# A hybrid decoder trunk: set-up sums kept in PSUM, a second raw weight buffer, GLA's score products in one run, later turns

## The chip, the cores and the metric

The kernel runs on one core of a Trainium2 chip. The metric is the device time of one execution, in microseconds (us). Each execution ends with the same output; the median of three is given, and one further execution was recorded by the hardware profiler. Engines are named as in the profile: PE (TensorE matmul), PEld (its weight loads), DVE (VectorE), ACT (ScalarE), POOL (GpSimd), SP (SyncE, which here issues most DMAs).

## The reference

One layer of a decoder trunk over 1024 tokens of width 1024, with four token mixers side by side on one normalised input:

```python
cond = jax.nn.silu(c)
shift, scale, gate = jnp.split(cond @ ada_w[l] + ada_b[l], 3, axis=-1)
u = _rms_norm(x, norm_g[l]) * (1 + scale[:, None]) + shift[:, None]
p = u @ w_in[l]
...
y_a = _rwkv7(...)     # A: delta-rule state update
y_b = _gla(...)       # B: gated linear attention
y_c = _mlstm(...)     # C: matrix memory
y_d = _hgrn2(...)     # D: gated linear recurrence
ys = jnp.stack([y_a * jax.nn.silu(rw_z), y_b * jax.nn.silu(gz),
                y_c * jax.nn.silu(mz), y_d * jax.nn.silu(hz)], axis=2).astype(dt)
branch = jnp.einsum('bsmv,mvd->bsmd', ys, w_branch[l])
gates = jax.nn.sigmoid(merge_logits).reshape(merge_logits.shape[:-1] + (N_BRANCH, D_MODEL))
merged = jnp.einsum('bsmd,bsmd->bsd', gates.astype(dt), branch)
x = x + gate[:, None] * (merged @ w_out[l])
return _rms_norm(x, final_g)
```

B and D share a chunked recurrence: per step S_t = diag(exp(log_g_t)) S_{t-1} + k_t v_t^T and o_t = S_t^T q_t. B (GLA) has 4 heads with keys of 64 and values of 128.

## The kernel before

Products in fp32 precision are made from three single-pass products: a weight `raw` tile is loaded, split by ACT into a rounded part `whi` (L303) and by DVE into the rest `wlo` (L304), and `mm3` (L314 to L316) issues hi x hi, hi x lo and lo x hi with 512 columns each. `project` does one 128-wide strip of `w_in` this way: 8 slices of 128 rows, 3 products each, for both halves of the sequence, 48 products in all. The raw tile has one buffer (`wraw`, L293, filled by SP at L297); `whi` and `wlo` have two each.

The program has these stages. **Set-up** (`make_u`, L153): x is normalised and transposed; then, for each of 8 slices j, `gather` (L220) forms the conditioning sums for shift and scale on DVE, as 8 operations on 128x256 tiles (L227 and L229) over `adaw`, which SP loads (L178). The sums of even and odd k go to two SBUF accumulators, four one-column products (L244) add them over partitions, L247 and L248 finish the slice's factors `ada` and `sD`, ACT makes `u` and its rounded part (L251, L252), POOL the rest `ul` (L253), and `chunk` multiplies the first two weight strips by it. Small parameter rows (`prow`, L107) are loaded meanwhile from ACT's queue, five behind each slice, and turned on PE at the end (L118, in `consts2`).

**Part one** is RWKV-7 (A), about 72 to 650 us, where SP first has sixteen loads `xd` (L385) that wait for a tile that POOL fills. **Part two** runs the units d0, b0, d1, c0, d2, b1, d3, c1 (HGRN2, GLA, mLSTM), each in four quarters of 256 tokens, with the projections of the next unit and gate projections between them, 650 to about 1490 us. Then come the merge and the output.

A quarter of a D or B unit first turns its values (`turn`, L922: PE transposes L927 into PSUM, ACT copies L932), forms the decayed keys `kt` in `carried` (ACT exponent, DVE L846), and turns those as well into `kT`. Products of `kT` and the values (L988 in D, L1131 in B) give what the chunk adds to the state. Then there are seven levels s = 64, 32, 16, 8, 4, 2, 1: ACT and DVE make a factor `lx`, DVE multiplies it by q (L1142 in B) and by k (L1145). For each chunk of 128 tokens PE then forms seven score products (L1154 in B, L1000 in D) and one for the tokens' own terms (L1156), DVE merges them into `AT` (L1162), and PE forms the output from the state (L1167) and from `AT` (L1171).

Which instruction comes next on an engine is decided by the Tile scheduler when the program is built: it orders each engine's stream by data and buffers, in program order where nothing else decides. `together` (L1302) emits a list of products with high priority and ties the later ones to the first, so that they stand as one run on PE. RWKV's scores (L619, L632) and D's scores are issued so; GLA's are not.

Of the kernel before, what the change touches and what calls it, by code (L numbers as in the profile page):

```python
# [18 lines left out]
P = 128  # L19
# [16 lines left out]
class Hybrid:  # L36
# [44 lines left out]
    def consts(self, sp):  # L81
# [17 lines left out]
        for name, ap, n in rows:  # L99
            if name in ("c", "mu"):  # L100
                o0, pr = o, sp.tile([P, P], F32, name=f"prow{o}")
            self.prow[name] = o
            if name == "conv":
                src = ap[0].rearrange("k (n p) -> (k n) p", p=P)
            else:
                src = ap.rearrange("a (n p) -> (a n) p", p=P)
            load = lambda d=pr[o - o0 : o - o0 + n, :], src=src: nc.scalar.dma_start(d, src)  # L107
            load() if o0 == 0 else self.loads.append(load)
            o += n
            if name == "ada_b":  # L110
                self.pturn(pr, 0, o)
# [41 lines left out]
    def make_u(self, first):  # L153
# [15 lines left out]
        for j in range(KC):  # L169

            if j in (1, 2):
                raw = self.wp.tile([P, KC, P], F32, tag="wraw", bufs=1, name="wraw0") if j == 1 else sp.tile([P, KC, P], F32, name="wraw1")
# [68 lines left out]
        for j in range(KC):  # L241
            for s in range(2):
                for z in range(2):
                    nc.tensor.matmul(aps[:, 8 * s + j : 8 * s + j + 1], lhsT=acc[z][:, s, :], rhs=self.one[:], start=z == 0, stop=z == 1)  # L244
# [14 lines left out]
            for _ in range(5):  # L259
                if self.loads:  # L260
                    self.loads.pop(0)()
# [7 lines left out]
    def gate_col(self, j):  # L269

        nc = self.nc
        w = self.wp.tile([P, KC, P], F32, tag="wraw", bufs=1, name=self.nm("gw"))
# [247 lines left out]
    def a_front(self, p, q):  # L520

        nc = self.nc
        r, k, v = (self.ast[p][n, q // 2][:, self.qsl(q)] for n in "rkv")
# [98 lines left out]
        self.together([lambda j=j, h=h: score(j, h) for j in range(4) for h in range(2)])  # L622
# [13 lines left out]
        self.together([lambda i=i: early(i // 2 % 2, 1 - i // 4, i % 2) for i in range(8)])  # L636
# [200 lines left out]
    def carried(self, c128, k):  # L837
# [9 lines left out]
        return f, self.turn(kt, "kT")  # L847
# [74 lines left out]
    def turn(self, src, name, cols=P, dst=None):  # L922
# [3 lines left out]
        for t in range(2):  # L926
            nc.tensor.transpose(pv[:, t * P : (t + 1) * P], src[:, t * P : (t + 1) * P], self.ident[:])  # L927
# [39 lines left out]
    def d_quarter(self, hd, qi, q, k, lg, v, sz, S):  # L967
# [4 lines left out]
        f, kT = self.carried(c128, k)  # L972
# [5 lines left out]
        for s in self.LV:  # L978
            x = self.level_factor(s, cs, lg)
            sp = lambda t: t[:, :QT].rearrange("p (b z t) -> p b z t", z=2, t=s)  # L980
            nc.vector.tensor_tensor(sp(x)[:, :, 1, :], sp(x)[:, :, 1, :], sp(q)[:, :, 1, :], ALU.mult)
# [134 lines left out]
    def b_quarter(self, pr, qi, q, k, lg, v, sz):  # L1116
# [3 lines left out]
        f, kT = self.carried(c128, k)  # L1120
# [6 lines left out]
        ps_ = self.iv()  # L1127
        for c in range(2):
            for h in range(2):
                hr = slice(64 * h, 64 * h + 64)  # L1130
                nc.tensor.matmul(ps_[hr, c * P : (c + 1) * P], lhsT=kT[:, c * P + 64 * h : c * P + 64 * h + 64],  # L1131
                                 rhs=V[h][:, c * P : (c + 1) * P], start=True, stop=True)
        Z, R = [], []
        for s in self.LV:
# [5 lines left out]
            for h in range(2):  # L1140
                hr = slice(64 * h, 64 * h + 64)
                nc.vector.tensor_tensor(r[hr, :, h, :].rearrange("p c (b t) -> p c b t", t=s), s5(x)[hr, :, :, 1, :],  # L1142
                                        s5(q)[hr, :, :, 1, :], ALU.mult)
# [5 lines left out]
        for c in range(2):  # L1149
            cc = slice(c * P, (c + 1) * P)  # L1150
            sc = [self.sc() for _ in range(2)]
            for li, s in enumerate(self.LV):
                lhs = (k if s == 1 else Z[li])[:, cc]
                nc.tensor.matmul(sc[li // 4][:, P * (li % 4) : P * (li % 4) + P], lhsT=lhs,  # L1154
                                 rhs=R[li][:, c].rearrange("p h t -> p (h t)"), start=True, stop=True)
            nc.tensor.matmul(sc[1][:, 384:386], lhsT=dg[:, cc], rhs=self.bo2[:], start=True, stop=True)  # L1156
# [145 lines left out]
    def together(self, fs):  # L1302

        with self.tc.high_priority():
            first = fs[0]()
            with self.tc.issue_after(first.ins):
                for f in fs[1:]:
                    f()

# [124 lines left out]
    def bload(self, m, d):  # L1434
# [3 lines left out]
        raw = self.wp.tile([P, KC, P], F32, tag="wraw", bufs=1, name=self.nm("wraw"))  # L1438
# [145 lines left out]

YT = 11
# [42 lines left out]
```

## Time and profile before

| what | value |
| --- | --- |
| median of 3 executions | 1787.57 us (1785.57 to 1788.39) |
| the profiled execution | 1786.18 us |
| its span in the trace | 1784.4 us |
| PE busy | 1695.0 us, 95% of the span |
| DVE, ACT, POOL busy | 65%, 42%, 19% |
| mean granted TensorE clock | 0.981 |
| read and written in HBM | 111.88 and 33.56 MB |

The profiled execution took 1.39 us less than the median. Its span ends 1.8 us short of its own time; the difference lies around the span. Busy shares are means over stages: PE is busy nearly everywhere but in the first 110 us, so what an edit is worth is read from the gaps of PE in the stage where the edit lies. The granted clock is 1.00 at PE's full speed.

### The profile page before, as it was taken

To read this page: it belongs to the slowest core of one execution; us is meant where nothing else is said; L and a number is where in the kernel's file an instruction comes from. 1 tells how busy PE (TensorE), PEld (TensorE's weight loads), DVE (VectorE), ACT (ScalarE), POOL (GpSimd) and SP (SyncE) were. 2 spreads that over 40 slices of the span, in tenths; PEclk is the share of its full clock that TensorE was granted. 3 is DMA by queue.
4 is the path that set the end of the run, shared out by engine and by line. 5 is a ranking of instruction groups with operands and counts; after the bars stand their busy time and mean duration, and the time that the engine had idled before them with its cause. 6 is when DMAs were issued, how large, how long until landed. Compare 5 with 4: busy or idle time off the path is not lost.

```text
span 1784.4 us, 28695 instructions
## 1 busy us (share of the span) xinstructions
PE 1695.0 (95%) x10515; PEld 1356.6 (76%) x10515; DVE 1164.9 (65%) x3173; ACT 753.7 (42%) x1780; POOL 330.3 (19%) x555
## 2 busy tenths in 40 slices
PE   5989999999999999999899999999899999999998
PEld 4767677777777778787677877887678888778886
DVE  7756868667667744856878545666887654576532
ACT  5633343343344336546534453546543443222221
POOL 4621111111111121000110001000010020276500
PEclk7989999999999999999999999999999999999999
DMA  9222222222221221221221212111112225676322
GB/s 298 59 75 46 52 71 73 50 70 57 60 77 43 66 66 48 60 66 39 57 60 42 77 39 74 60 54 39 57 36 62 60 75 182 225 232 193 136 91 75
DMA packets 224278, 147.30 MB, mean 83 GB/s; under 512 B 60511, under 2 KB 203018, under 8 KB 224138
## 3 DMA queue, kind: packets, MB, share of 16 engines
q1 hardware_dynamic: 208800, 109.23, 22.5%
q10 hardware_dynamic: 15338, 36.24, 5.7%
q8 instruction: 83, 1.36, 0.3%
q14 instruction: 57, 0.47, 0.1%
HBM read 111.88 MB, written 33.56 MB: 82 GB/s over the span
## 4 chain that ended last, share of the span: by engine, by line
PE 70%; DVE 15%; ACT 6%; POOL 3%; DMA 3%; issue 3%; SPq 0%; POOLq 0%; ACTq 0%; DVEq 0%
PE pj L314 13%; PE pj L315 13%; PE pj L316 13%; PE yw L738 3%; PE sc L689 3%; DMA wraw<-in_w_in_dram 2%; DVE adacc L229 2%; PE sc L1000 1%; PE pj L1472 1%; PE pj L1470 1%; PE pj L1471 1%; PE iv L1471 1%; PE iv L1472 1%; PE iv L1470 1%; DVE tm L676 1%
## 5 line engine op out<-in xcount | busy, mean ns | idle before, releaser
L314 PE MATMUL pj<-uh,whi 128*128 128x512 f32 x1344 | 547.0, 407 | 3.9 <-DVE rn L534 3.8
L315 PE MATMUL pj<-ul,whi 128*128 128x512 f32 x1344 | 540.6, 402 | 0.0
L316 PE MATMUL pj<-uh,wlo 128*128 128x512 f32 x1344 | 540.6, 402 | 0.0
L314 PEld LDWEIGHTS pj<-uh,whi 128*128 128x128 f32 x1344 | 255.4, 190 | 51.2 <-issue 5.5
L316 PEld LDWEIGHTS pj<-uh,wlo 128*128 128x128 f32 x1344 | 255.0, 190 | 48.4 <-issue 2.0
L315 PEld LDWEIGHTS pj<-ul,whi 128*128 128x128 f32 x1344 | 255.5, 190 | 45.7 <-issue 1.2
L303 ACT CAST whi<-wraw 128x1024 fp32r<-128x1024 f32 x89 | 93.0, 1045 | 227.0 <-PE pj L315 177.4
L304 DVE TENSOR_TENSOR wlo<-wraw,whi 128x1024 fp32r<-128x1024 f32 (+1 forms) x88 | 106.9, 1215 | 45.9 <-ACT whi L303 41.6
L888 POOL TENSOR_SCALAR ss<-ss 128x2 f32<-128x2 f32 x48 | 13.3, 278 | 565.7 <-ACT on L887 564.1
L676 DVE TENSOR_TENSOR tm<-nb,xr 32x1 f32<-32x1 f32 (+14 forms) x240 | 71.7, 299 | 5.8
L897 DVE SCALAR_TENSOR_TENSOR y<-yw,DV,z 128x256 f32<-128x256 f32 x48 | 22.2, 480 | 63.3 <-PE yw L895 62.9
L1416 ACT ACTIVATE g<-pj 128x512 f32<-128x512 f32 x64 | 38.0, 594 | 54.2 <-PE pj L316 46.0
L678 DVE TENSOR_REDUCE xr<-tm 32x1 f32<-32x1 f32 (+14 forms) x240 | 54.0, 225 | 6.4
L1480 POOL TENSOR_TENSOR acc<-acc,g 128x512 f32<-128x512 f32 x32 | 50.5, 1589 | 24.3 <-DVE g L1478 21.1
L535 POOL TENSOR_TENSOR rn<-rn,nhalf 128x4 f32<-128x4 f32 x16 | 19.6, 1222 | 178.7 <-DVE rn L534 178.7
L751 DVE SCALAR_TENSOR_TENSOR Gbd<-Gbd,fa,yw 64x64 f32<-64x64 f32 x128 | 35.6, 278 | 25.7 <-PE yw L738 23.9
L1471 PE MATMUL iv<-yt,whi 128*128 128x512 f32 x128 | 50.4, 394 | 1.6 <-DVE yt L1430 1.6
L1470 PE MATMUL iv<-yt,whi 128*128 128x512 f32 x128 | 50.2, 392 | 1.5 <-DVE acc L1475 0.7
L1470 PE MATMUL pj<-yt,whi 128*128 128x512 f32 x128 | 50.4, 394 | 0.0
L1471 PE MATMUL pj<-yt,whi 128*128 128x512 f32 x128 | 50.3, 393 | 0.0
L1472 PE MATMUL pj<-yt,wlo 128*128 128x512 f32 x128 | 50.2, 393 | 0.0
L1472 PE MATMUL iv<-yt,wlo 128*128 128x512 f32 x128 | 50.1, 391 | 0.0
(483 smaller groups left out, 3399.9 us busy)
## 6 DMA issues: line engine op xcount, KB each, us to landing
wraw<-in_w_in_dram SPq DMA_DIRECT2D x89, 512.0 KB
gdram<-g ACTq DMA_DIRECT2D x64, 256.0 KB
th<-gdram ACTq DMA_DIRECT2D x32, 512.0 KB
adaw<-in_ada_w_dram SPq DMA_DIRECT2D x16, 512.0 KB
ydram<-y SPq DMA_DIRECT2D x64, 128.0 KB
wraw<-in_w_branch_dram SPq DMA_DIRECT2D x16, 512.0 KB
yr<-ydram SPq DMA_DIRECT2D x32, 256.0 KB
x<-in_x_dram SPq DMA_DIRECT2D x8, 512.0 KB
```

The lines of the kernel that those rows point to most:

```text
L303: nc.scalar.copy(hi[:, :nk, :width], raw[:, :nk, :width])
L304: eng.tensor_tensor(lo[:, :nk, :width], raw[:, :nk, :width], hi[:, :nk, :width].bitcast(F32), ALU.subtract)
L314: nc.tensor.matmul(ps[:width, :], lhsT=a, rhs=xh[:, k, :], start=k == 0, stop=False)
L315: nc.tensor.matmul(ps[:width, :], lhsT=a, rhs=xl[:, k, :], start=False, stop=False)
L316: nc.tensor.matmul(ps[:width, :], lhsT=b, rhs=xh[:, k, :], start=False, stop=k == nk - 1)
L676: nc.vector.tensor_tensor(t2, n2[:, 0:i, i].unsqueeze(1).broadcast_to([32, i, i]), x2[:, 0:i, 0:i].rearrange("p j l -> p l j"), ALU.mult)
L678: nc.vector.reduce_sum(x2[:, i, 0:i], t2, axis=AX.X)
L689: mm = lambda o, l, r: nc.tensor.matmul(o, lhsT=l, rhs=r, start=True, stop=True)
L738: mm = lambda o, l, r, **kw: nc.tensor.matmul(o, lhsT=l, rhs=r, skip_group_check=True, **kw)
L1470: nc.tensor.matmul(pb[:], lhsT=bh[:, k, :], rhs=t[:, 0, :], start=k == 0, stop=False)
L1471: nc.tensor.matmul(pb[:], lhsT=bh[:, k, :], rhs=t[:, 1, :], start=False, stop=False)
L1472: nc.tensor.matmul(pb[:], lhsT=bl[:, k, :], rhs=t[:, 0, :], start=False, stop=k == 3)
```

## The change

Six things are altered.

1. `gather` keeps one accumulator per slice, in a PSUM bank, through seven operations; the eighth writes the sum to SBUF. Each operation then reads what the one before it wrote. Two one-column products per slice are left of four.
2. Every `wraw` tile has two buffers, where before there was one. The scratch for dynamic DMAs is cut from 1024 to 256.
3. The 14 parameter rows after the first three are loaded from SP's queue, behind the last `adaw`.
4. In D and B, `carried` returns the keys unturned. They are turned when the product of the level s = 32 has been emitted, and `behind` orders the turn after that product (for the schedule alone: nothing waits in the program for it). In B the four state products move along.
5. GLA's seven score products of a chunk and the one for own terms go through `together`, in reversed order: s = 1 first, s = 64 last.
6. RWKV's first two fronts are no longer tied (`TIE`).

```diff
@@ consts
-            load = lambda d=pr[o - o0 : o - o0 + n, :], src=src: nc.scalar.dma_start(d, src)
-            load() if o0 == 0 else self.loads.append(load)
+            load = lambda q, d=pr[o - o0 : o - o0 + n, :], src=src: q.dma_start(d, src)
+            load(nc.scalar) if o0 == 0 else self.loads.append(load)
@@ make_u, behind the loads of adaw
+        for load in self.loads:
+            load(nc.sync)
@@ gather
-                self.acc = [sp.tile([P, 2, P], F32, tag=f"adacc{z}", bufs=2, name=f"adacc{z}{j}") for z in range(2)]
+                self.acc = self.iv()[:, 0 : 2 * P].rearrange("p (s c) -> p s c", s=2)
+            acc = self.acc
             for k in ks:
-                w, acc = aw[j][:, k], self.acc[k % 2]
-                if k < 2:
-                    nc.vector.tensor_scalar(acc[:], w, self.cond[:, k : k + 1], None, ALU.mult)
-                else:
-                    nc.vector.scalar_tensor_tensor(acc[:], w, self.cond[:, k : k + 1], acc[:], ALU.mult, ALU.add)
-            return self.acc
+                w = aw[j][:, k]
+                if k == 0:
+                    nc.vector.tensor_scalar(acc, w, self.cond[:, k : k + 1], None, ALU.mult)
+                    continue
+                o = acc
+                if k == KC - 1:
+                    o = sp.tile([P, 2, P], F32, tag="adacc", bufs=2, name=f"adacc{j}")
+                nc.vector.scalar_tensor_tensor(o if k < KC - 1 else o[:], w, self.cond[:, k : k + 1], acc, ALU.mult, ALU.add)
+            return o
@@ make_u, column products
-                for z in range(2):
-                    nc.tensor.matmul(aps[:, 8 * s + j : 8 * s + j + 1], lhsT=acc[z][:, s, :], rhs=self.one[:], start=z == 0, stop=z == 1)
+                nc.tensor.matmul(aps[:, 8 * s + j : 8 * s + j + 1], lhsT=acc[:, s, :], rhs=self.one[:], start=True, stop=True)
...
-            for _ in range(5):
-                if self.loads:
-                    self.loads.pop(0)()
@@ wraw (also gate_col, bload and make_u's first strip)
-        raw = self.wp.tile([P, KC, P], F32, tag="wraw", bufs=1, name=self.nm("wraw"))
+        raw = self.wp.tile([P, KC, P], F32, tag="wraw", bufs=2, name=self.nm("wraw"))
@@ a_front
+        tie = (p, q) >= TIE
-        self.together([lambda j=j, h=h: score(j, h) for j in range(4) for h in range(2)])
+        self.together([lambda j=j, h=h: score(j, h) for j in range(4) for h in range(2)], tie)
@@ carried
-        return f, self.turn(kt, "kT")
+        return f, kt
@@ turn
+            i = nc.tensor.transpose(pv[:, t * P : (t + 1) * P], src[:, t * P : (t + 1) * P], self.ident[:])
+            if after is not None:
+                self.behind(i, after)
@@ d_quarter and b_quarter, in the loop over levels
+            if s == 32:
+                kT = self.turn(kt, "kT", after=i)
@@ b_quarter: the four state products stand there too, and the scores
-            for li, s in enumerate(self.LV):
-                lhs = (k if s == 1 else Z[li])[:, cc]
-                nc.tensor.matmul(...)
-            nc.tensor.matmul(sc[1][:, 384:386], lhsT=dg[:, cc], rhs=self.bo2[:], start=True, stop=True)
+            self.together([lambda li=li, s=s: level(li, s) for li, s in reversed(list(enumerate(self.LV)))] + [own])
@@ together and behind
+    def together(self, fs, tie=True):
+        with self.tc.high_priority() if tie else ExitStack():
             first = fs[0]()
+            with self.tc.issue_after(first.ins) if tie else ExitStack():
                 for f in fs[1:]:
                     f()
+    def behind(self, ins, other):
+        self.tc.add_manual_dep(ins.ins, other.ins.name,
+                               mybir.DependencyInfo(mybir.DependencyClass.NoSync, mybir.DependencyReason.DATA), reason="behind")
@@ constants
+TIE = (0, 2)
-    nc = _bacc.Bacc("TRN2", target_bir_lowering=False, num_devices=1, dynamic_dma_scratch_size=1024)
+    nc = _bacc.Bacc("TRN2", target_bir_lowering=False, num_devices=1, dynamic_dma_scratch_size=256)
```

What the scheduler makes of it is shown at three places. A row is a line of the program, an operation, and its output and inputs by name with a serial number; lines are 1 to 27 higher in the changed program.

The first place is SP's queue behind the set-up, before. `wraw_783` and `wraw_848` are the strips of the first RWKV projections, the sixteen `xd` loads wait for POOL, and `wraw_1072` is the next strip:

```order
L297 DMA wraw_783<-in_w_in_dram 128x8x128
L297 DMA wraw_848<-in_w_in_dram 128x8x128
L1038 DMA mlb<-in_ml_i_b_dram 4x1
L396 DMA up_729<-in_rw_w_up_dram 64x512 x2
L396 DMA up_738<-in_rw_a_up_dram 64x512 x2
L385 DMA xd_700<-NT_690 128x128 x8
L385 DMA xd_701<-NT_690 128x128 x8
L297 DMA wraw_1072<-in_w_in_dram 128x8x128
```

After, where the rows ahead of these are the 14 `prow` loads:

```order
L299 DMA wraw_767<-in_w_in_dram 128x8x128
L299 DMA wraw_832<-in_w_in_dram 128x8x128
L299 DMA wraw_1056<-in_w_in_dram 128x8x128
L1045 DMA mlb<-in_ml_i_b_dram 4x1
L398 DMA up_713<-in_rw_w_up_dram 64x512 x2
L398 DMA up_722<-in_rw_a_up_dram 64x512 x2
L387 DMA xd_684<-NT_674 128x128 x8
L387 DMA xd_685<-NT_674 128x128 x8
L299 DMA wraw_1482<-in_w_in_dram 128x8x128
```

The third strip has moved ahead of the sixteen loads that wait for POOL; the fourth one, `wraw_1482`, now stands right behind them.

The second place is PE in the first quarter of a GLA unit (`pj` rows are projections of the next unit, `iv` takes transposes and state products, `sc` scores), before:

```order
L315 MATMUL pj_9039<-ul_75,whi_9036 128x512
L316 MATMUL pj_9039<-uh_73,wlo_9035 128x512
L927 MATMUL iv_8896<-ident,kt_8890 128x128 x2
L314 MATMUL pj_9039<-uh_73,whi_9036 128x512
L315 MATMUL pj_9039<-ul_75,whi_9036 128x512
L316 MATMUL pj_9039<-uh_73,wlo_9035 128x512
L1131 MATMUL iv_8910<-V_8883,kT_8899 64x128
L1131 MATMUL iv_8910<-V_8888,kT_8899 64x128
L1131 MATMUL iv_8910<-V_8883,kT_8899 64x128
L1131 MATMUL iv_8910<-V_8888,kT_8899 64x128
L314 MATMUL pj_9039<-uh_73,whi_9036 128x512
L1167 MATMUL yw_8984<-Sbd_8308,qe_8905 128x256
```

Further on, still before, the score products stand singly between projections:

```order
L1154 MATMUL sc_8965<-Zr_8291,lx_8938 128x128
L316 MATMUL pj_9081<-uh_74,wlo_9035 128x512
L314 MATMUL pj_9081<-uh_74,whi_9036 128x512
L1154 MATMUL sc_8966<-Zr_8292,lx_8945 128x128
L315 MATMUL pj_9081<-ul_76,whi_9036 128x512
L1154 MATMUL sc_8966<-Zr_8293,lx_8952 128x128
L316 MATMUL pj_9081<-uh_74,wlo_9035 128x512
L1154 MATMUL sc_8966<-Zr_8294,k_8185 128x128
L1156 MATMUL sc_8966<-bo_584,dg_8908 128x2
```

After, at the same quarter's scores:

```order
L316 MATMUL pj_9065<-uh_74,whi_9020 128x512
L1163 MATMUL sc_8950<-Zr_8278,k_8169 128x128
L1163 MATMUL sc_8950<-Zr_8277,lx_8936 128x128
L1163 MATMUL sc_8950<-Zr_8276,lx_8929 128x128
L1163 MATMUL sc_8949<-Zr_8275,lx_8922 128x128
L1163 MATMUL sc_8949<-Zr_8274,lx_8915 128x128
L1163 MATMUL sc_8949<-Zr_8273,lx_8896 128x128
L1163 MATMUL sc_8949<-Zr_8272,lx_8889 128x128
L1167 MATMUL sc_8950<-bo_568,dg_8887 128x2
L317 MATMUL pj_9065<-ul_76,whi_9020 128x512
```

The eight products of the chunk stand in one run that begins with s = 1. Counted from the transposes of the values, the keys' turn stands behind 22, 20, 32 and 19 products of 512 columns in the four quarters of b0 where it stood behind 12, 11, 20 and 13, and the own product behind 40, 39, 51 and 38 where it stood behind 33, 37, 40 and 34. On PE, about 2018 rows in a row, which hold all of RWKV, are in the same order as before.

The third place is ACT ahead of the first mLSTM quarter (`fa`, `fc` and `dk` belong to the projection of the D unit d2, and `g` is a gate), before:

```order
L945 ACTIVATE fa_11232<-fa_11232 128x512
L949 ACT_TABLE_LOAD
L949 ACTIVATE fa_11232<-fa_11232 128x512
L948 ACT_TABLE_LOAD
L948 ACTIVATE fc_11233<-fc_11233 128x512
L950 ACT_TABLE_LOAD
L950 ACTIVATE fc_11233<-fc_11233,lbt 128x512
L952 ACT_TABLE_LOAD
L952 ACTIVATE dk_11235<-dk_11235 128x512
L1416 ACTIVATE g_11279<-pj_11254 128x512
```

After:

```order
L950 ACTIVATE fa_11216<-fa_11216 128x512
L953 ACTIVATE fc_11217<-fc_11217 128x512
L954 ACT_TABLE_LOAD
L954 ACTIVATE fa_11216<-fa_11216 128x512
L955 ACTIVATE fc_11217<-fc_11217,lbt 128x512
L957 ACT_TABLE_LOAD
L957 ACTIVATE dk_11219<-dk_11219 128x512
L1435 ACTIVATE g_11263<-pj_11238 128x512
```

Two of four table loads are gone there. In the whole program ACT has 29 of them where before there were 35.

## Rows read from the trace of the kernel before

**Rows 1.** The page, busy time, share and instructions of each engine.

```profile
PE 1695.0 (95%) x10515; PEld 1356.6 (76%) x10515; DVE 1164.9 (65%) x3173; ACT 753.7 (42%) x1780; POOL 330.3 (19%) x555
```

**Rows 2.** Waits of PE: engine, line, releaser: us in total, times, longest us.

```profile
PE sc L244 <- DVE adacc L229: 14.3, 5, 5.5
PE iv L927 <- DVE kt L846: 9.1, 9, 1.7
PE iv L1131 <- ACT kT L932: 4.2, 2, 2.2
PE pj L314 <- DVE rn L534: 3.8, 1, 3.8
```

**Rows 3.** Waits of ACT.

```profile
ACT whi L303 <- PE pj L315: 177.4, 57, 5.1
```

**Rows 4.** Windows: stretch, its length, each engine's busy us and instructions, granted clock, DMA.

```profile
26.95:63.07 36.12, 27.29 (x118) 22.67 (x119) 35.85 (x69) 20.68 (x30) 20.53 (x14) 0.74 0.64 163
63.07:72.55 9.48, 9.48 (x37) 7.60 (x36) 3.32 (x17) 3.75 (x6) 5.14 (x7) 0.82 0.21 57
94.90:107.40 12.50, 7.07 (x21) 5.11 (x21) 5.93 (x11) 5.55 (x11) 2.33 (x6) 0.59 0.33 88
```

**Rows 5.** Groups of DVE, 20 to 75 us: count, busy us, mean ns, idle before.

```profile
L229 DVE SCALAR_TENSOR_TENSOR adacc<-adaw,cond,adacc 128x256 f32<-128x256 f32 x48 | 33.7, 756 | 0.0
```

**Rows 6.** Timeline of DVE and POOL in the set-up: start us, us, count.

```profile
20.24 2.70 DVE L227 TENSOR_SCALAR adacc<-adaw,cond 128x256 f32<-128x256 f32 x2
27.21 1.27 DVE L229 SCALAR_TENSOR_TENSOR adacc<-adaw,cond,adacc 128x256 f32<-128x256 f32 x3
28.87 2.67 POOL L253 TENSOR_TENSOR ul<-u,uh 128x512 fp32r<-128x512 f32 x2 [6.34 <-ACT uh L252]
28.93 5.38 DVE L229 SCALAR_TENSOR_TENSOR adacc<-adaw,cond,adacc 128x256 f32<-128x256 f32 x3
```

**Rows 7.** Single lines of DVE: duration ns min/median/max, first and last start.

```profile
L785 DVE SCALAR_TENSOR_TENSOR t<-yw,DV,bv x16: 465/483/485, 195.8 to 659.7; 128x256 f32<-128x256 f32 x16
L1478 DVE SCALAR_TENSOR_TENSOR g<-th,pj x24: 672/684/689, 1557.4 to 1689.5; 128x512 f32<-128x512 f32 x24
```

**Rows 8.** Timeline of DVE, seven operations each on the last one's output.

```profile
853.66 2.68 DVE L280 SCALAR_TENSOR_TENSOR gacc<-gw,cond,gacc 128x128 f32<-128x128 f32 x7
```

**Rows 9.** Timeline of all engines at the start of RWKV.

```profile
84.22 7.48 SPq L385 DMA_DIRECT2D xd<-NT  x16
...
91.81 0.38 SPq L297 DMA_DIRECT2D wraw<-in_w_in_dram  x1
...
95.74 1.04 ACT L303 CAST whi<-wraw 128x1024 fp32r<-128x1024 f32 x1 [7.27 <-DMA wraw<-in_w_in_dram]
...
98.91 0.77 PE L314 MATMUL pj<-uh,whi 128*128 128x512 f32 x1 [3.76 <-DVE rn L534]
```

**Rows 10.** Timeline of PE and DVE, second quarter of b0.

```profile
853.73 0.60 PE L927 MATMUL iv<-ident,v 128*128 128x128 f32 x4
...
858.66 0.41 PE L927 MATMUL iv<-ident,kt 128*128 128x128 f32 x2 [1.48 <-DVE kt L846]
...
861.65 1.23 DVE L304 TENSOR_TENSOR wlo<-wraw,whi 128x1024 fp32r<-128x1024 f32 x1 [1.95 <-ACT whi L303]
...
869.58 0.58 DVE L1142 TENSOR_TENSOR Zr<-lx,q 64x128 f32<-64x128 f32 x2
...
871.39 0.28 PE L1156 MATMUL sc<-bo,dg 128*128 128x2 f32 x2
```

**Rows 11.** The same, first quarter of b0: values' turn, last level.

```profile
822.08 0.60 PE L927 MATMUL iv<-ident,v 128*128 128x128 f32 x4
...
833.75 0.58 DVE L1142 TENSOR_TENSOR Zr<-lx,q 64x128 f32<-64x128 f32 x2
```

**Rows 12.** Timeline of ACT and PE ahead of the first mLSTM quarter.

```profile
1068.89 1.28 ACT L952 ACT_TABLE_LOAD   x1
...
1072.68 0.44 PE L927 MATMUL iv<-ident,k 128*128 128x128 f32 x2 [3.76 <-ACT V L932]
```

More of the change, by code (lines that the diff above doesn't have):

```diff
@@ L171, in make_u @@
             if j in (1, 2):
-                raw = self.wp.tile([P, KC, P], F32, tag="wraw", bufs=1, name="wraw0") if j == 1 else sp.tile([P, KC, P], F32, name="wraw1")
+                raw = self.wp.tile([P, KC, P], F32, tag="wraw", bufs=2, name="wraw0") if j == 1 else sp.tile([P, KC, P], F32, name="wraw1")
                 nc.sync.dma_start(raw[:], self.win(first[j - 1]).rearrange("(k p) c -> p k c", p=P))
@@ L271, in gate_col @@
         nc = self.nc
-        w = self.wp.tile([P, KC, P], F32, tag="wraw", bufs=1, name=self.nm("gw"))
+        w = self.wp.tile([P, KC, P], F32, tag="wraw", bufs=2, name=self.nm("gw"))
         c0 = 2 * D + j * P
@@ L633, in early @@
                                     rhs=S_["VW"][kr, cp_, par, 64 * h : 64 * h + 64], start=True, stop=True)
-        self.together([lambda i=i: early(i // 2 % 2, 1 - i // 4, i % 2) for i in range(8)])
+        self.together([lambda i=i: early(i // 2 % 2, 1 - i // 4, i % 2) for i in range(8)], tie)
         Dw = S_["D"] = self.wk.tile([P, 2, P], F32, tag="Dw", bufs=3, name=self.nm("Dw"))
@@ L920, in qsl, with turn @@
         return slice((q % 2) * QT, (q % 2 + 1) * QT)
-    def turn(self, src, name, cols=P, dst=None):
+    def turn(self, src, name, cols=P, dst=None, after=None):
         nc = self.nc
@@ L971, in d_quarter @@
         V = self.turn(v, "V")
-        f, kT = self.carried(c128, k)
+        f, kt = self.carried(c128, k)
         cs = {n: self.cums(lg, n) for n in (64, 32)}
@@ L1119, in b_quarter @@
         V = [self.turn(v[j], "V") for j in range(2)]
-        f, kT = self.carried(c128, k)
+        f, kt = self.carried(c128, k)
         cs = {n: self.cums(lg, n) for n in (64, 32)}
@@ L1126, in b_quarter @@
         nc.gpsimd.tensor_tensor(dg[:, :QT], q, k, ALU.mult)
[L1127 to L1132, printed above, removed]
         Z, R = [], []
@@ L1141, in b_quarter @@
                 hr = slice(64 * h, 64 * h + 64)
-                nc.vector.tensor_tensor(r[hr, :, h, :].rearrange("p c (b t) -> p c b t", t=s), s5(x)[hr, :, :, 1, :],
-                                        s5(q)[hr, :, :, 1, :], ALU.mult)
+                i = nc.vector.tensor_tensor(r[hr, :, h, :].rearrange("p c (b t) -> p c b t", t=s), s5(x)[hr, :, :, 1, :],
+                                            s5(q)[hr, :, :, 1, :], ALU.mult)
+            if s == 32:
+                kT = self.turn(kt, "kT", after=i)
+                ps_ = self.iv()
+                for c in range(2):
+                    for h in range(2):
+                        hr = slice(64 * h, 64 * h + 64)
+                        nc.tensor.matmul(ps_[hr, c * P : (c + 1) * P], lhsT=kT[:, c * P + 64 * h : c * P + 64 * h + 64],
+                                         rhs=V[h][:, c * P : (c + 1) * P], start=True, stop=True)
             if s > 1:
@@ L1437, in bload @@
         f = lambda t: t[:].rearrange("p k c -> p (k c)").rearrange("p (k c) -> p k c", c=2 * P)
-        raw = self.wp.tile([P, KC, P], F32, tag="wraw", bufs=1, name=self.nm("wraw"))
+        raw = self.wp.tile([P, KC, P], F32, tag="wraw", bufs=2, name=self.nm("wraw"))
         lo = self.wp.tile([P, KC, P], F32R, tag="wlo", bufs=2, name=self.nm("wlo"))
```

13 lines of the change are left out of this document (6 added, 7 removed).

## The prediction

> **What bounds the kernel now.** I read the shares of busy time first: PE is busy for 1695.0 us, 95% of the span [rows 1]. What can be won is therefore mostly the idle time of PE, some 90 us, and the time in which it runs at the lower clock. The second view was PE's waits, which say where that idle time lies [rows 2]. Four of them are touched by the change: the one-column products of the set-up wait 14.3 us for DVE's sums, the transposes of `kt` 9.1 us for DVE, the state products behind them 4.2 us for ACT's copy of `kT`, and the projection at the start of RWKV 3.8 us for DVE's `rn`. The third view was ACT's waits: its casts of weights wait 177.4 us, in 57 cases, for PE to free the split tiles [rows 3]. In those cases the raw weights had landed, so an earlier load gains nothing there. The fourth view was the windows and the timeline of the stages in which PE idles; they price the terms.
>
> **Set-up sums.** Between the first and the last `sD`, 26.95 to 63.07 us, DVE is busy for 35.85 of 36.12 us and PE for 27.29 at a granted clock of 0.74 [rows 4]. DVE sets the pace. Its 48 accumulations take 33.7 us, 0.756 each [rows 5]. Three of them with POOL idle take 1.27 us, 0.42 each; three that begin beside POOL's `ul` and last into its next operation take 5.38, 1.79 each, and two of the other form take 2.70 beside POOL as well [rows 6]. So the sums are slow where both of an operation's tiles lie in SBUF and POOL works.
>
> The change makes one of the two tiles PSUM. Operations that read PSUM are not stretched: the 24 of L1478 take 0.672 to 0.689 us, in the merge, where POOL works too [rows 7]. At this shape a PSUM input costs 0.483 (L785) [rows 7]. No row shows DVE accumulate in PSUM. What the change takes away for it is the alternation: every operation now waits for the one before. Seven chained operations of half the width take 2.68 us, 0.383 each [rows 8]; 256 more elements cost about 0.20 (0.483 against 0.684), so 128 more cost 0.10, and a chained one at full width 0.48. I take 0.51, a little more, since the write to PSUM has no row. Below it lies 0.42, the alternating price; above it, 0.65 is what each costs now between the two `sD`: of 64 operations, 13 stand ahead of the first `sD`, so 51 lie in the 36.12 us, with 7 times 0.26 for the two small operations (26.95 to 27.21, rows 4 and 6) and 1.23 for a weight split, and (36.12 - 1.8 - 1.2) / 51 = 0.65. The new stretch is 51 x 0.51 + 3.0 = 29.0 us, 7.1 less. The 13 ahead of it take 6.6, as from 20.24 to 26.95 now: nothing there. PE must follow; it idled 8.8 us in the stretch, and behind it 9.48 us of its 9.48 are busy [rows 4], so these stay. I put **-7.0** (0 to -8.8). Half of the one-column products go; they lay in PE's idle time. The 14 parameter loads move from ACT's queue to SP's, behind `adaw`, ahead of the first RWKV strip. They are read only when the last `sD` is made, and the strip waited for its buffer anyway: 0.
>
> [...]
>
> **Second raw buffer.** In the RWKV stage and wherever the casts wait for PE [rows 3] it is worth 0. It counts where a load stood behind something in SP's queue. At the start of RWKV the third strip's load is issued at 91.81 us, behind sixteen `xd` loads from 84.22 to 91.7 that wait for POOL; ACT's cast starts at 95.74 after 7.27 us of waiting, and with it ACT and DVE are late for PE, which stands until 98.91 [rows 9]. The stretch from 94.90 to 107.40 has 7.07 us of PE work, at a clock of 0.59 [rows 4]. At full clock the work is 7.07 x 0.59 = 4.2 us, so 8.3 are lost. With the strip loaded ahead of the `xd` loads, that wait ends at ACT's and DVE's own work. The fourth strip is now behind the sixteen, and its cast may stand ahead of other work of ACT; I give back 2.0: **-6.3** (-2 to -8.3). It is late next if POOL's tile is.
>
> **Turn of keys and GLA's run.** The waits of 9.1 and 4.2 us, 13.3 together [rows 2], lie nearly all in the eight quarters of GLA. In the second quarter of b0 PE stands 1.48 us at 858.66 for `kt`, which is at the head of a quarter whose DVE also waits 1.95 for a weight's cast at 861.65 [rows 10]. With the turn 6 to 12 long products later, `kt` and `kT` have long been made: -13.3. The state products come later too, but DVE needs them only behind the scores.
>
> The run of eight makes a new wait. Its first product is that of s = 1, which DVE makes last. In this quarter that is at 869.58 + 0.58 = 870.16, 16.4 us behind the values' turn at 853.73, and PE reached the own product at 871.39, 17.7 behind it [rows 10]. Without the two waits (1.5 and 2.2) PE is there at 14.0, with two more projections and six score products fewer ahead at about 13. DVE without its 1.95 is ready at 14.4: a wait of 1.4. In the first quarter DVE is ready at 12.25 [rows 11], and PE with seven more projections ahead arrives at nearly the same time: 0.4. Half of the quarters like each, 4 x 1.8 = 7.2 come back. Behind the run wait the projections of the next unit, so the wait is PE's own loss. The run itself is worth 0, as eight products cost the same together. **-6.1** (-13.3 to +18, the second rival).
>
> **ACT ahead of mLSTM.** PE stands 3.76 us for ACT's copy of the values at 1072.68, behind four table loads of 1.28 [rows 12]. Two are gone in the new order: **-2.5** (0 to -2.6). The other four that go lie beside a busy PE: 0. D's later turns had hardly a wait: 0. RWKV's ties change no row on PE: 0. What the shifted order delays elsewhere has no row; waits of 1 to 2 us come and go when an order shifts, so I put +1 (-3 to +5). The smaller DMA scratch shows in no row either: 0.
>
> **Sum.** -7.0 - 6.3 - 6.1 - 2.5 + 1.0 = -20.9 us on the profiled execution's 1786.18, 1765.3. The median of the runs is 1.39 above that execution, so the median becomes **1767**.
>
> **Rivals.**
>
> 1. Sums in PSUM are slow. If each chained operation takes 0.65 us or more, the first term is 0 and the time 1774. For: the chain is strict, and no row shows the write. Against: the reads at 0.483, and that the chain of L280 runs at nearly its operations' length. [...] Chance 0.15.
> 2. GLA's run waits for DVE. If DVE keeps its times (16.4 and 12.25 us behind the values' turn [rows 10, 11]) while PE, rid of its waits, arrives at 10.1 and 10.6, the waits are 6.3 and 1.6, four times each 31.6 us, in place of 13.3. A wait of 3.76 was followed by the stretch at 0.59 [rows 9, 4], which cost 7.07 - 4.2 = 2.9 us; four more cost 11.6. The term turns from -6.1 to +18.3 + 11.6 = +29.9, and the time is 1803, slower. It decides from a mean wait of 3.5 us per quarter: 8 x 3.5 less 13.3 is then all that the other terms give, 14.8. For: nothing in the change makes DVE's levels any shorter. Against: the order puts two to eleven more projections ahead of the run, and DVE loses its own wait for weights. Chance 0.10.
> 3. Most of it does nothing: the third strip's early load meets a late `rn` all the same, and what the turns free is given back at the run. Then only the set-up counts: 1787.6 - 7.0 = 1781. For: RWKV's order is the same and the casts wait for PE. Against: the wait at 95.74 is for the DMA by name. Chance 0.12.
>
> **How the numbers follow.** The forecast has 0.58, with a range of its own of 1755 to 1775; 0.05 is left for a greater gain than that. The range of 1752 to 1783 takes in the forecast, the first rival and half of the third, some 0.8. A measurement of this kernel can tell about 0.2%, 3.6 us: faster is below 1784.0, slower above 1791.1. Faster: 0.58 + 0.05 + 0.15 + 0.06 (half of the third rival) = 0.84. Same: the other half, 0.06. Slower: the second rival, 0.10.
>
> **What would show it.** Right, step by step: the eight operations of a sum spaced by 0.5 us with no long ones, and the last `sD` near 56 us; no wait of ACT for the third strip, and PE at full clock from about 85 us on; no row of PE waiting at `kt` or `kT` in GLA; a new wait of PE at the first score of the run, for DVE, under 1 us in the mean; PE's wait at mLSTM's start near 1 us. Wrong: sums spaced by 0.65; a wait at the run of over 3 us in the mean; or a PE in RWKV whose gaps differ though its order doesn't.

## The result and the profile after

The changed kernel takes 1760.68 us in the median of four runs (1759.57 to 1763.87), against 1787.98 for the kernel before in the same comparison. The ratio is 0.9853, with an interval of 0.9834 to 0.9871: 27 us faster, where 21 were forecast and the range ended at 1752. The profiled execution has a span of 1758.3 us, 26.1 shorter than before.

The same point of the program, found in both traces, tells where they went. PE's first projection behind the set-up starts 5.1 us earlier (67.4 for 72.5). By 115 us it is 12.0, so the start of RWKV gives 6.9. All the rest of RWKV and D's first unit add 0.4. The GLA units give 3.2 (b0) and 1.1 (b1), the stretch around the second quarter of c0, the first mLSTM unit, 7.1, the merge 2.5; the end takes 0.9 back, and some 0.7 lie scattered. (The prediction and the texts of the experiments call that place the first mLSTM quarter; PE's wait there is at 1072.68 us, and c0's first quarter begins at 1042.67.)

PE's waits (engine, line, releaser: us in total, times, longest) and ACT's of the changed kernel:

```profile
PE sc L249 <- DVE adacc L235: 17.6, 6, 5.5
PE sc L1163 <- DVE Zr L1143: 4.9, 8, 1.5
PE yw L1181 <- DVE qe L1131: 4.7, 7, 1.5
PE yw L1185 <- DVE O L1187: 3.5, 2, 1.7
ACT whi L305 <- PE pj L317: 214.7, 69, 5.2
```

Of the four waits of [rows 2] three are gone; the fourth, for the set-up's sums, went from 14.3 to 17.6 us. New in GLA are the run's first product (eight waits, one per quarter), the product of the state with `qe`, and two for an output. ACT's casts now wait for PE 69 times where it was 57 [rows 3], and for their own load twice (7.4 us) where it was 12 times (36.5 us).

The windows that answer to [rows 4] (length, PE, PEld, DVE, ACT, POOL busy, granted clock, DMA):

```profile
27.29:59.37 32.08, 20.81 (x90) 16.54 (x91) 29.73 (x68) 20.58 (x30) 19.00 (x14) 0.80 0.83 214
59.37:67.43 8.06, 8.06 (x38) 6.58 (x36) 3.60 (x17) 3.86 (x6) 4.75 (x7) 1.00 0.00 0
89.78:95.40 5.62, 4.13 (x22) 3.02 (x22) 3.59 (x7) 2.73 (x5) 1.96 (x4) 1.00 0.54 137
```

The stretch between the first and the last `sD` is 32.08 us for 36.12; DVE is no longer busy all of it. The last `sD` comes 3.7 us earlier (59.37 for 63.07). The other 1.4 of the 5.1 lie behind it, where PE is busy throughout in both kernels: 8.06 us at a granted clock of 1.00, where it was 9.48 at 0.82 [rows 4]. The start of RWKV takes 5.62 for 12.50, at the full clock where 0.59 was granted. In the set-up's timeline, DVE's sums stand beside POOL's work, SP's loads and ACT's cast:

```profile
21.25 3.11 DVE L235 SCALAR_TENSOR_TENSOR iv<-adaw,cond,iv 128x256 f32<-128x256 f32 x6
...
31.83 2.33 DVE L253 SCALAR_TENSOR_TENSOR sD<-ada,PT 128x1 f32<-128x1 f32 x1
...
54.67 1.22 DVE L306 TENSOR_TENSOR wlo<-wraw,whi 128x1024 fp32r<-128x1024 f32 x1
55.80 0.48 DVE L235 SCALAR_TENSOR_TENSOR iv<-adaw,cond,iv 128x256 f32<-128x256 f32 x1
...
59.37 0.60 DVE L253 SCALAR_TENSOR_TENSOR sD<-ada,PT 128x1 f32<-128x1 f32 x1
...
21.16 2.34 POOL L306 TENSOR_TENSOR wlo<-wraw,whi 128x1024 fp32r<-128x1024 f32 x1 [3.13 <-ACT whi L305]
...
31.80 2.34 POOL L306 TENSOR_TENSOR w<-wraw,w 128x1024 fp32r<-128x1024 f32 x1
...
41.68 1.52 SPq L107 DMA_DIRECT2D prow<-in_rw_mu_dram  x1
...
48.95 7.33 SPq L299 DMA_DIRECT2D wraw<-in_w_in_dram  x3
```

Six accumulations take 3.11 us, most of them beside POOL's operation of 21.16, (3.11 - 0.49) / 5 = 0.52 apart: none is long any more, as against 1.79 each in [rows 6]. What is long is one `sD` of a single column, whose tensors `ada` and `PT` still both lie in SBUF: 2.33 us beside POOL's 2.34, with which it ends (34.16 and 34.14 us), where the first `sD`, at 27.48 with POOL idle, took 0.16. The split of the first RWKV strip (L306, 54.67) stands in DVE's order ahead of the last slice's last four operations.

### The profile page after: what moved, and what is told of

The parts are those of the page before. It is cut to its first block, busy times and chain, and to the rows that moved or that the text cites. A ratio compares the mean times of both kernels' runs of the same rounds, so it can differ in the third digit from the quotient of the medians.

```text
span 1758.3 us, 28549 instructions
## 1 busy us (share of the span) xinstructions
PE 1673.3 (95%) x10483; PEld 1344.4 (76%) x10483; DVE 1160.8 (66%) x3173; ACT 743.4 (42%) x1774; POOL 331.7 (19%) x555
## 4 chain that ended last, share of the span: by engine, by line
PE 67%; DVE 15%; ACT 6%; DMA 4%; POOL 4%; issue 3%; SPq 1%; POOLq 0%; DVEq 0%; ACTq 0%
PE pj L316 13%; PE pj L318 12%; PE pj L317 12%; PE yw L741 3%; PE sc L692 3%; PE sc L1007 2%; DVE tm L679 1%; PE sc L1163 1%; DVE wlo L306 1%; DMA yr<-ydram 1%; DVE c L837 1%; PE iv L1490 1%; PE pj L1489 1%; PE pj L1490 1%; PE pj L1491 1%
## 5 line engine op out<-in xcount | busy, mean ns | idle before, releaser
L306 DVE TENSOR_TENSOR wlo<-wraw,whi 128x1024 fp32r<-128x1024 f32 (+1 forms) x88 | 106.9, 1215 | 28.1 <-ACT whi L305 17.9
```

The lines of the kernel that those rows point to most:

```text
L306: eng.tensor_tensor(lo[:, :nk, :width], raw[:, :nk, :width], hi[:, :nk, :width].bitcast(F32), ALU.subtract)
```

## The experiments

Medians of different comparisons stand here beside the changed kernel's 1760.68; the kernel before had 1786.46 to 1788.27 in them. Where a median and a profile disagree by some us, the granted clock of the executions differs too (below), so the verdicts go by the point at which a trace falls behind or ahead.

PE's first projection behind the set-up is a poor mark of the set-up for the same reason. From the last `sD` to it PE is busy all the time in every trace, and that stretch took 8.0 to 8.2 us where the granted clock was 1.00 and 9.5 to 10.8 where it was 0.74 to 0.84. Four of the kernels below (one raw buffer, GLA untied, early turns, four table loads) have the same set-up as the changed kernel. Their last `sD` stands at 59.1 to 59.5 us, as its own does, but their first projection 1.3 to 2.4 later than its own. With GLA untied:

```profile
59.50:69.83 10.33, 10.33 (x37) 8.20 (x37) 1.69 (x17) 3.44 (x6) 4.25 (x7) 0.78 0.00 0
```

So the last `sD` is given beside the first projection.

**One raw buffer.** `bufs=2` to `bufs=1` at the four `wraw` tiles of the changed kernel.

> The changed kernel with one raw weight buffer instead of two. Theory (the second buffer carries the start of RWKV, most of the gain ahead of the first mLSTM quarter and the gain in the merge): about 1775 us, 14 later than the changed kernel, of which 6.9 are there by 115 us, 4 to 5 come between the first GLA unit and the first mLSTM quarter, 2.5 in the merge. Rival (the second buffer counts at the start of RWKV alone, the mLSTM gain is due to the two table loads that went): about 1768, with 6.9 by 115 us and nothing after.

Measured: 1779.14 us (1776.72 to 1783.63), ratio to before 0.9959 (0.9942 to 0.9975). Against the changed kernel it is 7.0 later in RWKV, 7.9 ahead of c0's second quarter, 14.8 behind it, 17.4 in the merge. PE stands 3.11 us for `rn` at 95.34 and 3.71 for ACT's copy again. The theory holds for the first two places, with 6.9 at the second where 4 to 5 were expected, and not for the merge: the 2.6 us between that quarter and the merge fall in and around the second GLA unit and have no account.

**The second buffer alone**, the kernel before with `bufs=2` and the smaller scratch.

> The kernel before with two raw weight buffers and the smaller scratch, nothing else. Theory (parts add up): about 14 us less than before, 1772 to 1774, of which 6 to 7 at the start of RWKV and the rest by the first mLSTM quarter; the waits at GLA's keys' turn shrink but stay. Rival (the second buffer needs the other edits, since the third strip is cast late anyway): less than 7 us.

Measured: 1767.90 us (1765.45 to 1772.99), ratio 0.9900 (0.9883 to 0.9916). Its trace is 8.5 earlier by 115 us, 10.1 ahead of c0's second quarter and 17.2 behind it: the two gains of the changed kernel, without any other edit. Of the 8.5, 1.5 are there at the first projection already; the last `sD` is no earlier (63.11), so they are the clock behind it. GLA's waits for `kt` did not shrink (9.8 us, 8 times). Two thirds of the whole gain are this one edit.

**Old sums.** The changed kernel with two SBUF accumulators and four column products.

```diff
-                self.acc = self.iv()[:, 0 : 2 * P].rearrange("p (s c) -> p s c", s=2)
+                self.acc = [sp.tile([P, 2, P], F32, tag=f"adacc{z}", bufs=2, name=f"adacc{z}{j}") for z in range(2)]
...
```

> The changed kernel with the set-up sums of before (two alternating SBUF accumulators, four column products). Theory: PE's first projection 5 us later than in the changed kernel, the rest unmoved, about 1766 us; DVE's sums with single operations over 1.5 us beside POOL again. Rival (the set-up's gain is the moved parameter loads, not the sums): about 1761, no more than 1 us later at the first projection.

Measured: 1767.42 us (1765.81 to 1770.13), ratio 0.9892 (0.9870 to 0.9914). The first projection is 3.4 later, less than the 5 expected, and so is the last `sD` (62.78); behind it the clock is 1.00 in both. The long operations are back: three take 5.38 us at 28.59. But the schedule is not otherwise the same: the split of the first RWKV strip stands behind the last `sD` here (68.49), ahead of it in the changed kernel (54.67). So 3.4 is what the sums save less what that split costs; the kernel with the strip late tells them apart. The trace is 7.9 later by 210 us, but the other 4.5 come in a stretch whose work is the same and whose clock is not (below).

**One accumulator in SBUF**, the chain kept.

```diff
-                self.acc = self.iv()[:, 0 : 2 * P].rearrange("p (s c) -> p s c", s=2)
+                self.acc = sp.tile([P, 2, P], F32, tag="adaccs", bufs=2, name=f"adaccs{j}")[:]
```

> The changed kernel with its one accumulator per slice in SBUF instead of PSUM, the chain kept. Theory (PSUM is what keeps the sums clear of POOL, the chain itself costs 0.1 us an operation): single operations of 1.5 to 2.6 us beside POOL again, undisturbed ones spaced by 0.52, the last factor sD at 65 us or later, the first projection 5 to 8 us later than in the changed kernel. Rival (fewer long ones since one accumulator is read where two were, and order alone matters): no operation over 1 us, first projection within 1 us.

Measured: 1771.97 us (1767.29 to 1774.67), last `sD` 9.1 later (68.43), first projection 10.7. Its DVE timeline:

```profile
26.35 2.05 DVE L235 SCALAR_TENSOR_TENSOR adaccs<-adaw,cond,adaccs 128x256 f32<-128x256 f32 x4
...
30.40 5.79 DVE L235 SCALAR_TENSOR_TENSOR adaccs<-adaw,cond,adaccs 128x256 f32<-128x256 f32 x4
```

Four chained operations take 2.05 us where POOL is idle, as in PSUM, and 5.79 beside POOL. (POOL's first `ul` begins 1.73 us behind the first `sD` in the kernel before and in the changed one; with that, an estimate, it begins at 30.2 us here.) So PSUM buys freedom from POOL, as four take 2.06 us at 29.67 in the changed kernel, beside POOL's `ul` from 29.21 on, and the chain costs the same in both memories. One accumulator in SBUF is worse than two (last `sD` 68.43 for 62.78, the strip's split behind it in both).

**Two accumulators in PSUM**, first in one bank:

> The changed kernel with two alternating accumulators per slice, both in one PSUM bank, and the four column products of before. Theory (the chain costs 0.12 us for each of 51 operations): operations spaced by 0.40 us, the last sD 4 to 6 us earlier, PE's first projection 2 to 5 us earlier than in the changed kernel, the whole 2 to 5 us less. Rival (the weights' arrival or PE's chunks become the bound at once): first projection within 1 us of the changed kernel.

Measured: 1762.14 us (1756.53 to 1766.74), last `sD` 0.7 earlier (58.67), first projection 1.6 later at a clock of 0.78. The spacing stayed 0.52, so this did not test what it was meant to; the run with two banks (below) did. That the scheduler ties the two halves of one bank to each other would explain it, but is not shown.

**Parameter loads earlier**, behind the sixth pair of condition weights:

> The changed kernel with the 14 parameter loads issued on SP behind the sixth pair of condition weights instead of behind the eighth. Theory (in the changed kernel these loads hold up the first RWKV strip's load, 41.7 to 48.9 us, whose cast on ACT and split on DVE stand in order ahead of the last sum): the strip's load is issued by 43 us, DVE waits for no cast before the last sum, PE's first projection 1 to 3 us earlier, the whole 1 to 3 us less than the changed kernel. Rival (the strip is not waited for in the end, PE's own work at the end of the set-up is the bound): within 0.5 us at the first projection.

Measured: 1762.57 us (1757.24 to 1765.69), last `sD` at 59.65, first projection 3.0 later, nearly all of it at the lower clock (0.74) behind that. DVE now waits 1.73 us for a condition weight behind those loads, and the strip, issued at 45.90 in place of 48.95, is cast no earlier (53.46, still waiting for its load). The theory falls: moving the loads moves the wait. **A combination** of these two with `sD` formed from the PSUM column came no further:

> The changed kernel with three edits: the parameter loads behind the sixth pair, two accumulators in one PSUM bank, and the factor sD formed from the PSUM column and two per-partition scalars, so that it has one SBUF input fewer and doesn't wait behind ada. Theory: no operation of DVE over 1 us between the first and last sD except the weight split, last sD near 52 us, first projection 5 to 8 us earlier than in the changed kernel, about 1754 to 1756 us. Rival (DMA brings the condition weights at a fixed rate, or PE's chunks bound the end): first projection no more than 3 us earlier, 1758 or more.

Measured: 1759.09 us (1757.99 to 1763.34), last `sD` at 59.25, first projection 2.5 later at a clock of 0.76. In all three the last `sD` stood at 58.7 to 59.7 us. In each of them, as in the four kernels with an unchanged set-up, DVE stands still ahead of the split of the first RWKV strip, for 0.4 to 2.0 us, because ACT's cast of it is late. In the kernel with GLA untied:

```profile
54.40 1.23 DVE L306 TENSOR_TENSOR wlo<-wraw,whi 128x1024 fp32r<-128x1024 f32 x1 [1.87 <-ACT whi L305]
```

In the changed kernel's own trace this wait does not show, as the `sD` of 2.33 us had made DVE late by then.

**The strip late.** The first RWKV strip's cast is ordered behind the last `uh`, its split behind the last `sD`:

```diff
+        if self.last is not None:
+            self.behind(a, self.last[1])
+            self.behind(b, self.last[0])
+            self.last = None
...
```

> The changed kernel, with the cast and split of the first RWKV strip ordered behind the last sD and the last uh. Theory (the split at about 54.5 us, waiting for that strip to land behind all the condition weights, stands in DVE's order ahead of the last sum and sets the end of the set-up): last sD near 55 us in place of 59.4, PE's first projection 1 to 4 us earlier than in the changed kernel, the whole 0 to 4 us less. Rival (PE's chunks, or the split itself when late, set the end): first projection within 1 us or later.

Measured: **1753.58 us** (1752.50 to 1753.86), ratio to before 0.9815 (0.9801 to 0.9828), whose interval lies below the changed kernel's. Its DVE timeline:

```profile
52.99 0.28 DVE L254 SCALAR_TENSOR_TENSOR sD<-ada,PT 128x1 f32<-128x1 f32 x1
55.61 0.61 DVE L254 SCALAR_TENSOR_TENSOR sD<-ada,PT 128x1 f32<-128x1 f32 x1
61.34 1.22 DVE L308 TENSOR_TENSOR wlo<-wraw,whi 128x1024 fp32r<-128x1024 f32 x1
```

The last `sD` is at 55.61, 3.5 to 3.9 earlier than in the five traces with the set-up of the changed kernel, and the first projection 3.7 earlier; the split at 61.34 is still in time for it at 63.7. Against the old sums, whose split stands behind the last `sD` as well, it is 62.78 - 55.61 = 7.2 earlier: that is what the new sums save (7.1 in the prediction's sum). This beats both kernels. Of the 7.1 us between its median and the changed kernel's the profiles give some 4 to the set-up and 1.4 to the stretch of 140 to 160 us, where this one had the full clock. **With all four edits**, and the two accumulators in two banks:

> The changed kernel with four edits in the set-up: parameter loads behind the sixth pair of condition weights, two alternating accumulators in two PSUM banks, sD from the PSUM column, and the first RWKV strip's cast and split behind the last sD. Theory (DVE's chain and the strip's split bound the set-up): operations spaced by 0.40 us between the banks, last sD near 50 us, first projection 4 to 7 us earlier than in the changed kernel, about 1755 us. Rival (operations that write PSUM are spaced by 0.52 whether they depend on each other or not, and PE's chunks set the end): spacing 0.52, first projection no more than 2 us earlier.

Measured: 1760.92 us (1754.34 to 1762.16), first projection 3.1 earlier. Its timeline:

```profile
20.18 2.26 DVE L222 TENSOR_SCALAR b<-PT 128x8 f32<-128x8 f32 x1
22.36 0.86 DVE L234 TENSOR_SCALAR iv<-adaw,cond 128x256 f32<-128x256 f32 x2
23.13 1.65 DVE L241 SCALAR_TENSOR_TENSOR iv<-adaw,cond,iv 128x256 f32<-128x256 f32 x4
```

In two banks four take 1.65 us, (1.65 - 0.47) / 3 = 0.39 apart: the chain's 0.12 is real. It gains nothing over the strip late alone: the last `sD` is at 56.17, as DVE waits 3.50 us for condition weights, which the parameter loads hold up, and the new small operation at 20.18 took 2.26 us (in the combination 2.24, where POOL has one operation, of 2.34 us, between 20 and 30 us). This kernel has the strip late too, and its profiled execution (1754.34) is like that one's; that its median is 7 us higher has no account but the clock, 0.992 in the profiled execution and 0.985 to 0.988 in the others.

**Early turns**, the keys turned in `carried` again, GLA's four state products moved back with them, GLA's run kept:

> The changed kernel with the keys turned at once, as before, in both GLA and HGRN2, and GLA's run kept. Theory: the waits of PE at the keys' turn and at the state products come back (13 us in total before, perhaps 8 with the second raw buffer), about 1766 to 1769 us, the whole difference in the GLA units. Rival (the second raw buffer removed those waits, since the waits were DVE's and ACT's for weights): within 2 us of 1761.

Measured: 1768.20 us (1765.71 to 1771.52), ratio 0.9896 (0.9873 to 0.9919). The GLA units are 2.9 and 1.8 longer; 4 more are lost at 140 to 160 us, at a clock of 0.66. **GLA untied**, keys late, `False` handed to `together` and the levels in the old order:

> The changed kernel with GLA's score products untied and in the order of before, keys still turned late. Theory (the run itself costs and saves nothing, the gain is the late turn): within 3 us of the changed kernel, 1758 to 1764, with no waits of PE at the keys' turn; the waits at the run's first product (4.9 us) go, and waits of the single products come. Rival (the run is what gains): about 1766, no gain left in the two GLA units.

Measured: 1765.85 us (1759.65 to 1766.76), ratio 0.9883 (0.9859 to 0.9908); its profiled execution, 1759.65, is 0.9 us behind the changed kernel at the merge, after +1.6 in b0 and -0.7 in b1. The run is worth no more than that in the traces, the late turn 4.7. The medians are 5 apart, though. The mean granted clock was 0.990 in the profiled execution and 0.985 to 0.986 in the three others; whether the run has to do with that stays open.

**Four table loads**, the exponent of unit d2 ordered behind its logarithm by `behind`, the second buffer kept:

> The changed kernel with the exponent of HGRN2's unit d2 ordered behind the logarithm, which brings back four table loads ahead of the first mLSTM quarter where the changed kernel has two; the second raw buffer stays. Theory (the gain there is the raw buffer's, through an earlier cast): PE's wait at the first mLSTM quarter under 1.5 us, that stretch within 2 us of the changed kernel. Rival (the two table loads made the wait of 3.76 us and the lower clock behind it): the wait is back at 3 us or more and the stretch 5 to 7 us longer.

Measured: one execution of 1771.86 us. Between the points at 1025.9 and 1069.6 of the changed kernel it loses 7.8. Twenty us from the same place on in the kernel before, in the changed one and in this one:

```profile
1060.00:1080.00 20.00, 15.12 (x65) 11.35 (x63) 9.30 (x25) 14.02 (x20) 0.00 (x0) 0.83 0.29 86
```

```profile
1044.40:1064.40 20.00, 19.43 (x103) 15.91 (x102) 12.03 (x34) 13.24 (x28) 1.19 (x2) 1.00 0.29 86
```

```profile
1052.00:1072.00 20.00, 14.30 (x63) 10.97 (x63) 8.04 (x20) 14.42 (x20) 0.00 (x0) 0.83 0.28 84
```

With the loads back, PE is idle 5.7 us of 20 and the clock is at 0.83. The rival holds in the length of the stretch: the table loads make this loss, and the second buffer counts there, it seems, because with it the scheduler finds the order with fewer (ahead of the quarter four again with one buffer, two with two). It does not hold in the place: PE waits 1.83 and 2.40 us for ACT ahead of the quarter and only 1.46 at it. The edit also brings in more than it takes back: eight table loads between c0's first and second quarter, where the kernel before had six and the changed one four. So 7.8 is rather too much for the two loads alone.

## Why the prediction was right, and where its sizes were off

**Set-up, -7.0 forecast, -5.1 measured.** The mechanism and the price of the sums held: they are spaced by 0.52 where 0.51 was put, none is long, they save 7.2 us where nothing else holds DVE, and rival 1 (0.65) fell. Chained operations took 0.52 in both memories and alternating ones 0.39 to 0.40 in both; the operation that begins a sum, with one tensor input, took 0.48 with its output in PSUM and 0.35 with it in SBUF. (The 0.42 that the prediction sets against L785's 0.483 is the mean of three overlapping operations; one alone takes 0.476 in the kernel before.)

The sign that failed is the last `sD`, at 59.4 instead of "near 56". The step that failed is "the strip waited for its buffer anyway: 0". In the kernel before, the first strip's load was issued right behind the last condition weight, and its cast waited for nothing; only the second strip waited for a buffer. In the changed kernel the 14 parameter loads stand between, the strip is issued at 48.95, and its split, which stands ahead of the last sum, comes late. With one buffer it is no earlier (49.20). The load in the kernel before, the cast in the kernel before, and the load in the kernel with one buffer:

```profile
42.27 2.12 SPq L297 DMA_DIRECT2D wraw<-in_w_in_dram  x1
...
52.47 1.03 ACT L303 CAST whi<-wraw 128x1024 fp32r<-128x1024 f32 x1
...
49.20 6.45 SPq L299 DMA_DIRECT2D wraw<-in_w_in_dram  x2
```

The late strip showed what it cost, some 3.7 us. No run put the 14 loads back on ACT's queue, so what they alone cost is not shown. A second step failed the other way, by luck: the 9.48 us behind the last `sD` do not "stay", they were at a clock of 0.82 and became 8.06 at 1.00.

**Start of RWKV, -6.3 forecast, -6.9 measured.** Right in place and size, as both runs on the buffer show; the fourth strip's cast (91.09, behind the sixteen `xd` loads) cost PE one wait of 1.49 us. The first half of rival 3 (a late `rn` all the same) fell with the second buffer alone.

**GLA, -6.1 forecast, -4.3 measured.** The 13.3 us of waits went and 4.9 came at the run, under the 7.2 allowed: in the first quarter of b0 0.80, in the second 0.32, so rival 2 (6.3 and 1.6) fell. What the sum missed is what is late next: the product of the state with `qe` (4.7 us) and two of the output products behind it (3.5 us), both at nothing in the prediction:

```profile
822.83 0.49 PE L1163 MATMUL sc<-Zr,k 128*128 128x128 f32 x2 [0.80 <-DVE Zr L1143]
...
855.98 0.49 PE L1163 MATMUL sc<-Zr,k 128*128 128x128 f32 x2 [0.32 <-DVE Zr L1143]
...
872.52 0.67 PE L1181 MATMUL yw<-Sbd,qe 128*128 128x256 f32 x2 [1.54 <-DVE qe L1131]
```

With these PE stands still as long as before, and the second half of rival 3 is nearly true: what the turns free is given back, though only a part of it at the run. The stretch around b0, before and after:

```profile
815.00:950.00 135.00, 126.38 (x697) 99.13 (x697) 104.80 (x306) 74.74 (x200) 11.12 (x22) 0.99 0.17 49
```

```profile
802.59:934.37 131.78, 122.50 (x697) 98.64 (x697) 104.34 (x306) 70.67 (x198) 10.92 (x23) 1.00 0.17 50
```

PE's idle time is 8.62 us before and 9.28 after; the 3.2 us of gain are in its busy time, for the same 697 products, at a clock of 0.99 and 1.00. Around b1 it is 11.97 idle before and 12.90 after, at 0.98 in both, and why PE was busy for less there stays open. So the term came near its size in part by luck. That the late turn is worth something all the same shows in the early turns: with the run kept, turning the keys at once makes PE stand still for 11.8 us around b0 instead of 9.28.

**ACT ahead of mLSTM, -2.5 forecast, -7.1 measured.** This is the term that was mis-sized. The cause, two table loads fewer, was right, as the run with four showed for the length of the stretch; I took its worth from the loads' own 2.56 us. The wait of 3.76 was followed by two more and by a granted clock of 0.83, and all of it went: PE waits 0.57 us there now.

**Elsewhere, +1 forecast, -2.7 measured.** In the merge 2.2 us are gained at one place. 1.6 of them are the clock: a wait of 1.30 us is there in both, and the products behind it took 0.63 us in the kernel before, at a granted clock of 0.52 (1605.7 to 1609.2 us), and 0.40 in the changed one, at 1.00 (1580.0 to 1582.4). The other 0.6 is a wait of 0.52 us just ahead of it that only the kernel before has.

The terms missed in both directions: set-up and GLA gave 3.7 us less than forecast, the other three 8.9 more. That the sum missed by only 5.2 of 26.1 us is partly luck.

## What to carry to other kernels

Ask of a load that is moved or doubled what stands behind its cast and split on their engines: a split that is not yet needed, placed ahead of a sum that is, cost 3.7 us here. A stall can be worth the whole stretch up to the point where the clock is back, not its own length alone: here one of 3.76 us, with two more and a clock of 0.83 behind it, was worth 7.1. When waits go, count the engine's whole idle time before and after, as new waits can take their place: in GLA 13.3 us of waits went, and PE stood still no less. Where DVE and POOL work side by side, try one of DVE's two inputs in PSUM: here four sums took 5.79 us beside POOL with both in SBUF and 2.06 with one in PSUM. Two accumulators in two banks bring the spacing from 0.52 to 0.39 us, which won no time here.

## What the runs showed of the hardware

The same wait of 1.8 us for `XY` at about 140 us was followed by the full clock in some executions and by a lower one in others, though PE's products ahead of it stand in the same order. The wait with GLA untied and with old sums:

```profile
140.50 0.68 PE L692 MATMUL sc<-XY,NT 64*64 64x64 f32 x16 [1.78 <-DVE XY L715]
```

```profile
142.11 0.68 PE L689 MATMUL sc<-XY,NT 64*64 64x64 f32 x16 [1.84 <-DVE XY L712]
```

The windows of 140 to 160 us of the same two:

```profile
140.00:160.00 20.00, 19.50 (x208) 14.79 (x208) 12.38 (x35) 6.03 (x14) 0.24 (x1) 1.00 0.24 53
```

```profile
140.00:160.00 20.00, 18.16 (x113) 13.51 (x112) 10.37 (x27) 5.46 (x11) 0.00 (x0) 0.66 0.12 24
```

PE issued 208 products in the one and 113 in the other, from places in the program 1.6 us apart. It is worth 4 to 5 us of a run, more than most edits here, and shows only in the windows: a difference of that size between two kernels is read stage by stage before it is given to an edit. The kernel with the strip late kept the full clock there, and its four runs lie within 1.4 us; that its narrow spread comes from this was not tested.
